# A hybrid decoder layer: scratch laid out with 32 or 128 rows outermost, more projection buffers, stores issued from GpSimd

## The chip, the cores and the metric

The kernel runs on one core of a Trainium2 chip. A core has engines that run in parallel, each through its own list of instructions in order: TensorE (PE, matrix products into the accumulator memory PSUM), VectorE (DVE), ScalarE (ACT), GpSimd (POOL) and SyncE (SP), which here only issues transfers (DMA). An instruction that waits holds up all that stand behind it on its engine. The metric is device time in microseconds (us); less is better.

## The reference

One layer over 1024 positions of 1024 channels, with 16 learned meta rows ahead (1040 in all), in float32:

```python
h_res = h_res + 0.5 * swiglu_ffn(rmsnorm(h_res, ffn1_norm), w_gate1, w_up1, w_down1)   # 1024 -> 2816 -> 1024
proj  = rmsnorm(h_res, mix_norm) @ w_in            # 1024 -> 2560
q, k, v, u = split(proj, [512, 1024, 1536])
a = diff_attention(rope(q), rope(k), v)            # 4 heads x 2 maps of 64; p0 - lam * p1; per-head norm
c = silu(layernorm(causal_depthwise_conv31(glu(u))))
h_res = h_res + concat([a, c]) @ w_out
h_res = h_res + 0.5 * swiglu_ffn(rmsnorm(h_res, ffn2_norm), w_gate2, w_up2, w_down2)
y = rmsnorm(h_res, final_norm)[16:]
```

## The kernel before

Channels lie on the 128 partitions and positions along the free axis. The sequence goes in two halves: half 1 has 528 columns (the meta rows and 512 positions, in two blocks of 264), half 2 has 512. Every product is made of three matmuls on float32r numbers: operands are split into a high and a low part (`split`, L125 to L127: the high part a copy on ScalarE, the low part a subtraction on VectorE). A weight tile of 512 KB is loaded by SyncE into `wraw` (2 buffers), and split into `whl` (4 buffers).

The stages follow one another: first feed-forward of half 1 (0 to 398 us); projections of half 1 (`project`, L600); first feed-forward of half 2, with the attention and the convolution of half 1 as pieces between its steps (`mixer`, L750); projections of half 2, with half 1's output projection inside them; second feed-forward of half 1 with half 2's attention and convolution between its steps; half 2's output projection; and half 2's second feed-forward.

`project` makes first four tiles of the convolution's gated input (L619 to L642), then the rotary keys and queries (`rope`, L649, groups of four sub-heads), then the values (L685). Keys, queries and values go through scratch in DRAM, since attention wants them in another layout. A block of keys or queries takes 48 matmuls into two PSUM tiles (`pa`, `pb`), four multiplications by the cosine and sine tables (`t`, L661), a difference and a sum (L666, L667), a split into the tile `pk` (one buffer, L654), and the store: one transfer of `pk` for keys (L674, scratch side ordered row, part, column; 128 rows outermost), four for queries (L680, each 4 sub-heads x 32 rows x columns, four outermost). Values take 24 matmuls a tile of 128 positions (`pv`), are scaled and split into `ve` (two buffers, L695 and L140/L141), and stored at L697. Attention loads the keys of a sub-head at L396, read from scratch as 4 parts x 32 rows x columns with the four outermost, the queries at L399, the values at L490. A head's score products (`sc`) go into a PSUM tile with one buffer, which the reduction of its maximum (L428) and the exponential into `p` (L437) must have read before the next one starts.

PSUM for all projections and feed-forward tiles comes from one pool of five (`psG`, L69). The sum of squares and the split of the next stage's input into `xh` and `xl` (`enter`, L279) are ordinary instructions of ScalarE and VectorE; `xh` is one buffer that each stage overwrites. Other trips through scratch: x after the first feed-forward (`xscr`, L342), the norm's factors by token (`rtok`, L614), and attention's and convolution's results (`rscr` L511, `acscr` L522).

A scheduler fixes the order on each engine before the run, from priorities and the buffers that are free. All transfers, loads and stores, are issued by SyncE in one order, so a store that waits for ScalarE's result holds up the loads behind it.

Of the kernel before, what the change touches and what calls it, by code (L numbers as in the profile page):

```python
# [9 lines left out]
F32 = mybir.dt.float32  # L10
# [39 lines left out]
def layer(ctx, tc, xb, wgu1, wd1, win, wv, wo, wgu2, wd2, colv, lamv, consts, cossin, out):  # L50
    nc = tc.nc
    V, S, T = nc.vector, nc.scalar, nc.tensor
    dma = nc.sync.dma_start

    def mm(o, lhsT, rhs, start, stop):
        T.matmul(o, lhsT, rhs, start=start, stop=stop)  # L56
# [14 lines left out]
    psB = ctx.enter_context(tc.tile_pool(name="psB", bufs=1, space=PSUM))  # L71
    dram = ctx.enter_context(tc.tile_pool(name="dscr", bufs=1, space=DRAM))

    kscr = dram.tile([4, 8, 32, L], F32, tag="kscr", name="kscr")
    qscr = dram.tile([8, 2, 64, SEQ], F32, tag="qscr", name="qscr")
    vscr = dram.tile([L, 4, 2, P], F32, tag="vscr", name="vscr")
    xscr = dram.tile([2, P, ND, HB], F32, tag="xscr", name="xscr")
    rtok = dram.tile([2, HM], F32, tag="rtok", name="rtok")
# [186 lines left out]
                        down_piece(hls[d // 2], n, d % 2, d, hs, c0, w)  # L265
                        after(c0, w, d)

# [1 line left out]
    def rms(x, c0, w):  # L269
        ssum = tmp.tile([P, 512], F32, tag="ssum", name="ssum")  # L270
        for d in range(ND):
# [58 lines left out]
    def mix_in(b, x):  # L330
        sums = {}

        def f(c0, w, d):
            if d == 0:
                sums[c0] = tmp.tile([P, 512], F32, tag="ssum", name="ssum")
            xs = x[:, d, c0:c0 + w]
            gain_piece(xs, col(C_GM + d), xh[:, d, c0:c0 + w], xl[:, d, c0:c0 + w])
            sq_piece(xs, w, sums[c0], d == 0)
            if d == ND - 1:
                norm_r(rB[:, c0:c0 + w], w, sums[c0], 95 if c0 + w == FB[b][-1][0] + FB[b][-1][1] else 60)  # L340
                a = max(c0, RO[b])
                dma(xscr[b][:, :, a - RO[b]:c0 + w - RO[b]], x[:, :, a:c0 + w])  # L342
        return f

    cst = const.tile([P, 2 * P], F32, tag="cst", name="cst")
# [18 lines left out]
        V.tensor_scalar(lnh, cols[:, C_LG:C_LG + 8], 0.5, None, op0=ALU.mult)  # L364
        V.tensor_scalar(wsub, col(C_SUB), 1.0 - LAM_INIT, None, op0=ALU.mult)

# [1 line left out]
    class Mid:  # L368
        pass

# [22 lines left out]
    def load_qk(m, sub):  # L393
        b, nk = m.b, m.nk
        k = m.qk.tile([P, nk], F32R, tag="k", name="k")
        dma(k.bitcast(F32), kscr[:, sub, :, :nk])  # L396
        q = m.qk.tile([P, 2, HB], F32R, tag="q", name="q")
        for rep in range(2):
            dma(q[64 * rep:64 * rep + 64].bitcast(F32),  # L399
                                qscr[sub, :, :, HB * b:HB * b + HB].rearrange("h r c -> r h c"))  # L400
        return k, q

    def unit(m, i, kq, ptiles, half):
# [98 lines left out]
    def sub_ln(m):  # L502
        v = psb("v")
        for h in range(4):
            sq = tmp.tile([P, 512], F32, tag="sq", name="sq")
            S.activation(sq, m.os[h], AF.Square)
            mm(v[32 * h:32 * h + 32], onesH, sq, True, True)
        rr = tmp.tile([P, 512], F32, tag="ssum", name="rr")
        rstd(v, rr, 512)
        for h in range(4):  # L510
            dma(rscr[m.b, h:h + 1], rr[32 * h:32 * h + 1])  # L511
        for h in range(4):
            ra = tmp.tile([P, 512], F32, tag="ssum", name="ra")
            dma(ra, rscr[m.b, h].partition_broadcast(P))
            V.scalar_tensor_tensor(ra, m.os[h], wsub, ra, op0=ALU.mult, op1=ALU.mult)
            store_ac(m, h, ra)

    def store_ac(m, i, src):
        hi, lo = [tmp.tile([P, HB], F32R, tag="rs", name="a") for _ in range(2)]
        split(hi, lo, src)  # L520
        for j, t in enumerate((hi, lo)):
            dma(acscr[m.b, i, :, j], t.bitcast(F32))  # L522

    def conv(m, c, z):
        a = zp.tile([P, ZH], F32, tag="z", name="acc")[:, :HB]
# [70 lines left out]
                V.tensor_tensor(x[:, d, :HB], ps, x[:, d, :HB], op=ALU.add)  # L596
                after(d)

# [1 line left out]
    def project(b, zs, between):  # L600
        es = ExitStack()
        tp = pool(es, f"tp{b}", 2)
        N = HM if b == 0 else HB
        g0 = 0 if b == 0 else HM
        ro = RO[b]
        cs = tp.tile([P, 2, N], F32, tag="cs", name="cs", bufs=1)
        dma(cs, cossin[:, :, g0:g0 + N])
        wt = WT[b]

        toks = ([(0, NM)] if b == 0 else []) + [(ro + P * t, P) for t in range(4)]  # L610
        rcol = tp.tile([P, 5], F32, tag="rcol", name="rcol", bufs=1)

        def token_rstd():
            dma(rtok[b:b + 1, :N], rB[0:1, :N])  # L614
            if b == 0:
                dma(rcol[:NM, 0:1], rtok[b, 0:NM].rearrange("(p t) -> p t", t=1))
            dma(rcol[:, len(toks) - 4:len(toks)], rtok[b, ro:N].rearrange("(t p) -> p t", p=P))

        for c in range(4):  # L619
            if c == 3:  # L620
                token_rstd()
            hg = load_w(win[2 * c + 1])
            ha = load_w(win[2 * c])
            z = zp.tile([P, ZH], F32, tag="z", name="z")
            if b == 0:
                V.memset(z[:, :ZH - HM], 0.0)
            else:
                V.tensor_copy(z[:, :CW - 1], zh[:, c])
            for c0, w in FB[b]:
                rb = rB[:, c0:c0 + w]  # L630
                pg = psg("pg")[:, :w]
                proj(pg, hg, c0, w)
                t = tp.tile([P, wt], F32, tag="t", name="t", bufs=4)[:, :w]
                V.tensor_tensor(t, pg, rb, op=ALU.mult)
                S.activation(t, t, AF.Tanh, scale=0.5)
                V.scalar_tensor_tensor(t, t, 1.0, rb, op0=ALU.add, op1=ALU.mult)
                pa = psg("pa")[:, :w]
                proj(pa, ha, c0, w)
                V.scalar_tensor_tensor(z[:, ZH - N + c0:ZH - N + c0 + w], pa, 0.5, t, op0=ALU.mult, op1=ALU.mult)
            if b == 0:  # L640
                V.tensor_copy(zh[:, c], z[:, HB:ZH])
            zs.append(z)  # L642

        between()

        for i in range(2):
            V.tensor_tensor(cs[:, i], cs[:, i], rB[:, :N], op=ALU.mult)

        def rope(wi, blocks, scale, store):  # L649
            ha = load_w(win[wi])  # L650
            hb = load_w(win[wi + 1])
            for c0, w in blocks:
                co, si = cs[:, 0, c0:c0 + w], cs[:, 1, c0:c0 + w]
                pk = tp.tile([P, 4, wt], F32R, tag="pk", name="pk", bufs=1)  # L654

                def part(hl, name):
                    ps = psg(name)[:, :w]
                    proj(ps, hl, c0, w)
                    t = [tp.tile([P, wt], F32, tag="t", name="t", bufs=4)[:, :w] for _ in range(2)]
                    for u, tab in zip(t, (co, si)):  # L660
                        V.scalar_tensor_tensor(u, ps, scale, tab, op0=ALU.mult, op1=ALU.mult)  # L661
                    return t

                ac, as_ = part(ha, "pa")
                bc, bs = part(hb, "pb")
                V.tensor_tensor(ac, ac, bs, op=ALU.subtract)  # L666
                V.tensor_tensor(bc, bc, as_, op=ALU.add)  # L667
                split(pk[:, 0, :w], pk[:, 2, :w], ac)
                split(pk[:, 1, :w], pk[:, 3, :w], bc)
                store(c0, w, pk.bitcast(F32))  # L670

        for g in range(2):
            def store_k(c0, w, pk):
                dma(kscr[:, 4 * g:4 * g + 4, :, g0 + c0:g0 + c0 + w].rearrange("k s r c -> (s r) k c"), pk[:, :, :w])  # L674

            def store_q(c0, w, pk):
                q0 = HB * b + c0 - ro
                for hl in range(2):
                    for ab in range(2):
                        dma(qscr[4 * g:4 * g + 4, hl, 32 * ab:32 * ab + 32, q0:q0 + w], pk[:, 2 * hl + ab, :w])  # L680

            rope(8 + 4 * g, FB[b], 1.0, store_k)
            rope(10 + 4 * g, QB[b], 0.125, store_q)

        for vh in range(2):  # L685
            hv = [load_w(wv[2 * vh + i]) for i in range(2)]
            for t, (c0, n) in enumerate(toks):
                ps = psg("pv")[:n, :256]
                for k in range(ND):
                    o = (k % 4) * 256  # L690
                    wh, wl = hv[k // 4][:, 0, o:o + 256], hv[k // 4][:, 1, o:o + 256]
                    mm(ps, xh[:, k, c0:c0 + n], wh, k == 0, False)
                    mm(ps, xh[:, k, c0:c0 + n], wl, False, False)
                    mm(ps, xl[:, k, c0:c0 + n], wh, False, k == ND - 1)
                ve = tp.tile([P, 2, 2, P], F32R, tag="ve", name="ve")  # L695
                gain_piece(ps.rearrange("p (a c) -> p a c", a=2), rcol[:n, t:t + 1], ve[:n, :, 0], ve[:n, :, 1])
                dma(vscr[g0 + c0:g0 + c0 + n, 2 * vh:2 * vh + 2], ve[:n].bitcast(F32))  # L697
        es.close()

    def after_out(x):  # L700
# [70 lines left out]
    def nothing(*_):  # L771
        pass

# [1 line left out]
    # keeps the tensor engine's clock up until the first operands are there  # L775
    awake = psb("awake")
    for _ in range(10):
        mm(awake[:, :P], onesD, onesD, True, True)
# [134 lines left out]
```

## Time and profile before

| | us |
|---|---|
| median of 3 runs | 2002.03 (2001.81 to 2005.81) |
| span of the profiled execution | 2003.7 |
| TensorE busy in it | 1948.8 (97%) |
| VectorE busy | 1319.8 (66%) |
| ScalarE busy | 698.6 (35%) |
| GpSimd busy | 0.2, four instructions |

The span runs from the first instruction's start to the last one's end. A busy share is over the whole span, whose stages differ: of TensorE's idle time the view by stage tells more. Rows of waits name the instruction that waited, the arrow, and what ended the wait. PEclk is the clock granted to TensorE as a share of its full speed of 2.4 GHz.

### The profile page before, as it was taken

To read this page: it belongs to the slowest core of one execution; us is meant where nothing else is said; L and a number is where in the kernel's file an instruction comes from. 1 tells how busy PE (TensorE), PEld (TensorE's weight loads), DVE (VectorE), ACT (ScalarE), POOL (GpSimd) and SP (SyncE) were. 2 spreads that over 40 slices of the span, in tenths; PEclk is the share of its full clock that TensorE was granted. 3 is DMA by queue.
4 is the path that set the end of the run, shared out by engine and by line. 5 is a ranking of instruction groups with operands and counts; after the bars stand their busy time and mean duration, and the time that the engine had idled before them with its cause. 6 is when DMAs were issued, how large, how long until landed. Compare 5 with 4: busy or idle time off the path is not lost.

```text
span 2003.7 us, 27079 instructions
## 1 busy us (share of the span) xinstructions
PE 1948.8 (97%) x10772; PEld 1682.9 (84%) x10772; DVE 1319.8 (66%) x2112; ACT 698.6 (35%) x1163; POOL 0.2 (0%) x4
## 2 busy tenths in 40 slices
PE   9999999998899999999999799999999999999997
PEld 9999999998788888788878678787878878888886
DVE  8555555766588877766565677877775684544556
ACT  5222222432343333534232444343443332222223
POOL 0000000000000000000000000000000000000000
PEclk9999999999999999999999899999999999999999
DMA  5322323354634533265425443435248343332331
GB/s 174 96 86 86 94 90 91 112 160 132 190 103 111 128 104 97 79 228 183 156 90 172 155 106 105 116 95 127 74 132 275 96 129 96 94 95 91 97 97 63
DMA packets 92947, 240.71 MB, mean 120 GB/s; under 512 B 9322, under 2 KB 26474, under 8 KB 92692
## 3 DMA queue, kind: packets, MB, share of 16 engines
q1 hardware_dynamic: 92820, 238.97, 39.9%
q8 instruction: 85, 1.39, 0.3%
q14 instruction: 42, 0.34, 0.1%
HBM read 209.43 MB, written 29.51 MB: 119 GB/s over the span
## 4 chain that ended last, share of the span: by engine, by line
PE 88%; DMA 6%; DVE 3%; ACT 2%; issue 0%; SPq 0%; ACTq 0%; DVEq 0%
PE pg L56 27%; PE pu L56 24%; PE dn L56 23%; PE wo L56 4%; PE pa L56 4%; DMA qscr<-pk 2%; PE sc L56 2%; DMA vscr<-ve 1%; DMA wraw<-wd 1%; PE o L56 1%; PE pb L56 1%; DMA kscr<-pk 1%; PE v L56 1%; PE tm L463 1%; DVE whl L127 1%; ACT whl L126 1%
## 5 line engine op out<-in xcount | busy, mean ns | idle before, releaser
L126 ACT CAST whl<-wraw 128x1024 fp32r<-128x1024 f32 (+2 forms) x329 | 337.2, 1026 | 760.6 <-PE dn L56 204.8
L56 PE MATMUL pg<-xh,whl 128*128 128x512 f32 (+1 forms) x1936 | 526.9, 352 | 12.0 <-ACT xh L126 9.5
L56 PE MATMUL dn<-h,whl 128*128 128x512 f32 (+2 forms) x2736 | 510.6, 346 | 0.0
L127 DVE TENSOR_TENSOR whl<-wraw,whl 128x1024 fp32r<-128x1024 f32 (+2 forms) x329 | 392.8, 1195 | 163.0 <-ACT whl L126 161.9
L56 PEld LDWEIGHTS dn<-h,whl 128*128 128x128 f32 x2736 | 431.8, 189 | 65.1 <-issue 1.0
L56 PE MATMUL pu<-xh,whl 128*128 128x512 f32 (+1 forms) x1744 | 475.7, 352 | 0.0
L56 PEld LDWEIGHTS pg<-xh,whl 128*128 128x128 f32 x1936 | 343.4, 190 | 63.1 <-ACT xh L126 9.9
L56 PEld LDWEIGHTS pu<-xh,whl 128*128 128x128 f32 x1744 | 308.1, 189 | 49.0 <-issue 4.2
L56 PE MATMUL pg<-xl,whl 128*128 128x512 f32 (+1 forms) x968 | 339.6, 352 | 0.0
L56 PE MATMUL pu<-xl,whl 128*128 128x512 f32 (+1 forms) x872 | 305.3, 351 | 0.0
L232 DVE SCALAR_TENSOR_TENSOR x<-dn,x 128x512 f32<-128x512 f32 (+2 forms) x248 | 139.8, 571 | 99.2 <-PE dn L56 98.8
L56 PEld LDWEIGHTS pg<-xl,whl 128*128 128x128 f32 x968 | 183.0, 190 | 24.7 <-DVE xl L127 1.1
L56 PEld LDWEIGHTS pu<-xl,whl 128*128 128x128 f32 x872 | 163.5, 188 | 22.7 <-issue 0.8
L533 DVE SCALAR_TENSOR_TENSOR acc<-z,cols,acc 128x512 f32<-128x512 f32 x240 | 179.4, 747 | 3.3
L218 DVE TENSOR_TENSOR t<-pu,t 128x512 f32<-128x512 f32 (+1 forms) x109 | 64.1, 589 | 92.3 <-PE pu L56 89.5
L210 DVE TENSOR_TENSOR t<-pg,rA 128x264 f32<-128x264 f32 (+1 forms) x65 | 33.7, 520 | 92.6 <-PE pg L56 92.6
L56 PE MATMUL pa<-xh,whl 128*128 128x264 f32 (+2 forms) x384 | 91.2, 322 | 1.7 <-DVE t L661 1.7
L56 PE MATMUL wo<-acl,whl 128*128 128x512 f32 x384 | 89.9, 395 | 0.0
L56 PEld LDWEIGHTS wo<-acl,whl 128*128 128x128 f32 x384 | 72.1, 188 | 17.5
L126 ACT CAST h<-t 128x512 fp32r<-128x512 f32 (+1 forms) x110 | 58.6, 534 | 53.8 <-DVE t L218 53.6
L56 PE MATMUL pv<-whl,xh 128*128 128x256 f32 (+1 forms) x288 | 56.7, 299 | 17.8 <-DVE ve L141 9.5
L56 PEld LDWEIGHTS pa<-xh,whl 128*128 128x128 f32 x384 | 64.6, 188 | 8.4 <-DVE t L661 1.9
(153 smaller groups left out, 1576.3 us busy)
## 6 DMA issues: line engine op xcount, KB each, us to landing
wraw<-wgu SPq DMA_DIRECT2D x175, 512.0 KB
wraw<-wd SPq DMA_DIRECT2D x64, 512.0 KB
wraw<-win SPq DMA_DIRECT2D x32, 512.0 KB
wraw<-wd SPq DMA_DIRECT2D x32, 384.0 KB
q<-qscr SPq DMA_DIRECT2D x32, 256.0 KB
acscr<-a SPq DMA_DIRECT2D x32, 256.0 KB
acl<-acscr SPq DMA_DIRECT2D x16, 512.0 KB
wraw<-wo SPq DMA_DIRECT2D x16, 512.0 KB
```

The costliest lines, as they stand in the source:

```text
L56: T.matmul(o, lhsT, rhs, start=start, stop=stop)
L126: S.copy(dst_hi, src)
L127: return V.tensor_tensor(dst_lo, src, dst_hi.bitcast(F32), op=ALU.subtract)
L210: V.tensor_tensor(tw, pg, rb, op=ALU.mult)
L218: V.tensor_tensor(tw, pu, tw, op=ALU.mult)
L232: last[0] = V.scalar_tensor_tensor(xs, m[:, :w], 0.25, xs, op0=ALU.mult, op1=ALU.add)
L463: T.transpose(tm[:, j], ps_[0][:, o:o + P], ident)
L533: V.scalar_tensor_tensor(a, z[:, j:j + HB], col(wc + j), a, op0=ALU.mult, op1=ALU.add)
```

## The change

Three things are done. The scratch of keys is now ordered sub-head, part, 32 rows, columns, and so is that of queries, so a sub-head's keys are read as 128 rows, and both are stored in four transfers a block, one for each sub-head, with 32 rows outermost. The buffers `pk` (now two) and `ve` (now four) come from a pool of their own, opened after `between()`. And all stores to scratch (`xscr`, `rtok`, `kscr`, `qscr`, `vscr`, `rscr`, `acscr`) are issued by GpSimd; loads and the kernel's output stay on SyncE. Lines after the first are one higher in the changed kernel (L54 is new), from L647 on more.

```diff
     dma = nc.sync.dma_start
+    store = nc.gpsimd.dma_start
...
-    kscr = dram.tile([4, 8, 32, L], F32, tag="kscr", name="kscr")
-    qscr = dram.tile([8, 2, 64, SEQ], F32, tag="qscr", name="qscr")
+    kscr = dram.tile([8, 4, 32, L], F32, tag="kscr", name="kscr")
+    qscr = dram.tile([8, 4, 32, SEQ], F32, tag="qscr", name="qscr")
...
-                dma(xscr[b][:, :, a - RO[b]:c0 + w - RO[b]], x[:, :, a:c0 + w])
+                store(xscr[b][:, :, a - RO[b]:c0 + w - RO[b]], x[:, :, a:c0 + w])
...
-        dma(k.bitcast(F32), kscr[:, sub, :, :nk])
+        dma(k.bitcast(F32), kscr[sub, :, :, :nk].rearrange("k r c -> (k r) c"))
...
             dma(q[64 * rep:64 * rep + 64].bitcast(F32),
-                                qscr[sub, :, :, HB * b:HB * b + HB].rearrange("h r c -> r h c"))
+                qscr[sub, :, :, HB * b:HB * b + HB].rearrange("(h a) r c -> (a r) h c", h=2))
...
-            dma(rscr[m.b, h:h + 1], rr[32 * h:32 * h + 1])
+            store(rscr[m.b, h:h + 1], rr[32 * h:32 * h + 1])
...
-            dma(acscr[m.b, i, :, j], t.bitcast(F32))
+            store(acscr[m.b, i, :, j], t.bitcast(F32))
...
-            dma(rtok[b:b + 1, :N], rB[0:1, :N])
+            store(rtok[b:b + 1, :N], rB[0:1, :N])
...
         between()
 
+        rp = pool(es, f"rp{b}", 2)
...
-        def rope(wi, blocks, scale, store):
+        def rope(wi, blocks, scale, spill):
...
-                pk = tp.tile([P, 4, wt], F32R, tag="pk", name="pk", bufs=1)
+                pk = rp.tile([P, 4, wt], F32R, tag="pk", name="pk", bufs=2)
...
-                store(c0, w, pk.bitcast(F32))
+                spill(c0, w, pk.bitcast(F32))
...
             def store_k(c0, w, pk):
-                dma(kscr[:, 4 * g:4 * g + 4, :, g0 + c0:g0 + c0 + w].rearrange("k s r c -> (s r) k c"), pk[:, :, :w])
+                for s in range(4):
+                    dst = kscr[4 * g + s, :, :, g0 + c0:g0 + c0 + w]
+                    store(dst.rearrange("k r c -> r k c"), pk[32 * s:32 * s + 32, :, :w])
 
             def store_q(c0, w, pk):
                 q0 = HB * b + c0 - ro
-                for hl in range(2):
-                    for ab in range(2):
-                        dma(qscr[4 * g:4 * g + 4, hl, 32 * ab:32 * ab + 32, q0:q0 + w], pk[:, 2 * hl + ab, :w])
+                for s in range(4):
+                    dst = qscr[4 * g + s, :, :, q0:q0 + w]
+                    store(dst.rearrange("k r c -> r k c"), pk[32 * s:32 * s + 32, :, :w])
...
-                ve = tp.tile([P, 2, 2, P], F32R, tag="ve", name="ve")
+                ve = rp.tile([P, 2, 2, P], F32R, tag="ve", name="ve", bufs=4)
                 gain_piece(ps.rearrange("p (a c) -> p a c", a=2), rcol[:n, t:t + 1], ve[:n, :, 0], ve[:n, :, 1])
-                dma(vscr[g0 + c0:g0 + c0 + n, 2 * vh:2 * vh + 2], ve[:n].bitcast(F32))
+                store(vscr[g0 + c0:g0 + c0 + n, 2 * vh:2 * vh + 2], ve[:n].bitcast(F32))
```

The order of the transfers on SyncE in half 1's projections before, from the first load of keys on (`wv` and `wgu` are weights, `k` and `q` the loads for attention; x4 means four in a row):

```order
L396 DMA k<-kscr 128x1x528
L680 DMA qscr<-pk 4x32x256 x4
L396 DMA k<-kscr 128x1x528
L680 DMA qscr<-pk 4x32x256 x2
L108 DMA wraw<-wv 128x1024
L680 DMA qscr<-pk 4x32x256 x2
L108 DMA wraw<-wv 128x1024
L399 DMA q<-qscr 64x2x512
L674 DMA kscr<-pk 128x4x264
```

And after the change:

```order
L109 DMA wraw<-win 128x1024 x8
L109 DMA wraw<-wv 128x1024 x2
L397 DMA k<-kscr 128x528 x2
L109 DMA wraw<-wv 128x1024 x2
L400 DMA q<-qscr 64x2x512 x4
L109 DMA wraw<-wgu 128x1024 x6
L491 DMA vt<-vscr 128x4x256
```

The stores are gone from this list; the loads of weights now stand with only loads of scratch between them. The stores of half 1 stand on GpSimd, after the change:

```order
L343 DMA xscr<-x 1024x1x248
L343 DMA xscr<-x 1024x1x264
L615 DMA rtok<-rB 16x1x33
L678 DMA kscr<-pk 32x4x264 x8
L684 DMA qscr<-pk 32x4x256 x8
L678 DMA kscr<-pk 32x4x264 x8
L684 DMA qscr<-pk 32x4x256 x8
L701 DMA vscr<-ve 16x512
L701 DMA vscr<-ve 128x512 x4
```

There were none on this engine before. The second place is the end of half 2's projections on ScalarE. Before, with `ve` the values' high part, `xh` the feed-forward's input, `th` the tanh of the first gate tile and `p` the exponential of the scores:

```order
L140 ACTIVATE ve<-pv,rcol 128x2x128 x4
L126 CAST xh<-xs 128x512 x3
L126 CAST whl<-wraw 128x1024 x2
L140 ACTIVATE ve<-pv,rcol 128x2x128
L126 CAST xh<-xs 128x512 x5
L126 CAST whl<-wraw 128x1024
L437 ACTIVATE p,sm<-sc,nm 128x656
L207 ACTIVATE th<-pg 128x512
```

And after the change:

```order
L127 CAST xh<-xs 128x512 x4
L127 CAST whl<-wraw 128x1024
L208 ACTIVATE th<-pg 128x512
L141 ACTIVATE ve<-pv,rcol 128x2x128 x4
L127 CAST whl<-wraw 128x1024
L127 CAST h<-t 128x512
L127 CAST whl<-wraw 128x1024
L208 ACTIVATE th<-pg 128x512
L127 CAST whl<-wraw 128x1024
L127 CAST h<-t 128x512
L438 ACTIVATE p,sm<-sc,nm 128x656
```

The last four `ve` have moved behind the first gate tile's `th`, and the first exponential `p` behind the second gate tile's `h`. On VectorE at the same place, after the change (`acc` are convolution steps, `t<-th,pg` the gate's product):

```order
L209 SCALAR_TENSOR_TENSOR t<-th,pg 128x512
L534 SCALAR_TENSOR_TENSOR acc<-z,cols,acc 128x512 x2
L142 SCALAR_TENSOR_TENSOR ve<-pv,rcol,ve 128x2x128
L534 SCALAR_TENSOR_TENSOR acc<-z,cols,acc 128x512
L142 SCALAR_TENSOR_TENSOR ve<-pv,rcol,ve 128x2x128 x2
```

Before, the last `ve` there stood among the low parts of `xh`, ahead of all convolution steps; now two of these and the gate's product stand ahead of the first of the last four.

## Rows read from the trace of the kernel before

**Rows 1.** The page, busy time: engine, us (share of the span) and instructions.

```profile
PE 1948.8 (97%) x10772; PEld 1682.9 (84%) x10772; DVE 1319.8 (66%) x2112; ACT 698.6 (35%) x1163; POOL 0.2 (0%) x4
```

**Rows 2.** Windows, three stages: us, busy (count) per engine, clock, DMA share, GB/s.

```profile
460.00:545.00 85.00, 72.51 (x548) 68.00 (x548) 45.85 (x97) 23.74 (x44) 0.00 (x0) 0.94 0.55 171
...
1030.00:1130.00 100.00, 83.48 (x420) 71.21 (x419) 55.94 (x84) 27.19 (x40) 0.00 (x0) 0.90 0.49 154
1130.00:1475.00 345.00, 334.78 (x1615) 276.48 (x1613) 272.69 (x405) 146.96 (x260) 0.00 (x0) 0.99 0.40 109
```

**Rows 3.** Windows, stretches at half clock: the first, the last, the sum of seven.

```profile
499.50:502.91 3.41, 3.21 (x16) 2.17 (x17) 2.54 (x6) 0.00 (x0) 0.00 (x0) 0.50 0.98 291
...
1376.73:1380.14 3.41, 3.41 (x10) 2.67 (x9) 3.41 (x5) 0.93 (x3) 0.00 (x0) 0.50 0.70 161
sum 37.52, PE 30.19 PEld 24.80 DVE 26.58 ACT 19.10 POOL 0.00; mean PE 4.31 PEld 3.54 DVE 3.80 ACT 2.73 POOL 0.00
```

**Rows 4.** Waits of TensorE, 460 to 545 us: total us, times, longest.

```profile
PE pg L56 <- ACT xh L126: 5.9, 1, 5.9
PE pv L56 <- DVE t L661: 4.9, 1, 4.9
```

**Rows 5.** Waits of TensorE, 1030 to 1130 us.

```profile
PE pv L56 <- DVE ve L141: 9.5, 1, 9.5
PE pg L56 <- ACT xh L126: 3.6, 1, 3.6
```

**Rows 6.** Waits of TensorE, 1130 to 1475 us.

```profile
PE sc L56 <- ACT p L437: 10.2, 3, 3.8
```

**Rows 7.** Waits of ScalarE, 460 to 545 us.

```profile
ACT pk L126 <- DMA qscr<-pk: 21.7, 3, 9.1
ACT pk L126 <- DMA kscr<-pk: 12.4, 3, 4.3
```

**Rows 8.** Waits of ScalarE, 1030 to 1130 us.

```profile
ACT ve L140 <- DMA vscr<-ve: 19.4, 3, 13.4
```

**Rows 9.** The chain that ended last: start us, us, what was waited for.

```profile
470.08 4.96 DMA kscr<-pk
478.05 8.76 DMA qscr<-pk
...
1180.82 13.95 DMA wraw<-wd
```

**Rows 10.** DMA issues: destination, source, queue, count, KB each.

```profile
k<-kscr SPq DMA_DIRECT2D x8, 520.0 KB
...
kscr<-pk SPq DMA_DIRECT2D x4, 528.0 KB
...
qscr<-pk SPq DMA_DIRECT2D x16, 128.0 KB
```

**Rows 11.** Timeline of ScalarE: start us, us, instruction, [idle before, releaser].

```profile
419.05 0.63 ACT L131 ACTIVATE ssum<-x 128x512 f32<-128x512 f32 x1 [2.96 <-DMA x<-xb]
...
443.01 1.05 ACT L126 CAST whl<-wraw 128x1024 fp32r<-128x1024 f32 x1 [4.96 <-PE pg L56]
...
1185.17 0.59 ACT L207 ACTIVATE th<-pg 128x512 f32<-128x512 f32 x1
...
1194.85 1.05 ACT L126 CAST whl<-wraw 128x1024 fp32r<-128x1024 f32 x1 [6.43 <-DMA wraw<-wd]
1195.80 0.61 ACT L126 CAST h<-t 128x512 fp32r<-128x512 f32 x1
```

**Rows 12.** Windows, two blocks of keys in the first projections.

```profile
449.51:461.13 11.62, 11.62 (x98) 11.62 (x97) 11.09 (x19) 3.16 (x5) 0.00 (x0) 1.00 0.29 85
```

**Rows 13.** Timeline of VectorE at 1186 us.

```profile
1186.44 0.68 DVE L208 SCALAR_TENSOR_TENSOR t<-th,pg 128x512 f32<-128x512 f32 x1
```

**Rows 14.** The page, groups: VectorE convolution steps, busy, mean ns, idle before.

```profile
L533 DVE SCALAR_TENSOR_TENSOR acc<-z,cols,acc 128x512 f32<-128x512 f32 x240 | 179.4, 747 | 3.3
```

**Rows 15.** SyncE, issues of the stores of q: ns least/median/most, first to last.

```profile
L680 SPq DMA_DIRECT2D qscr<-pk x24: 503/552/4317, 475.8 to 1096.8; - x24
```

## The prediction

> **What bounds the kernel now.** I read the busy table first. TensorE is busy 1948.8 us of the span, so at most the rest and the cost of a halved clock can be won by anything but fewer matmuls; GpSimd does four set-up instructions and nothing else [rows 1]. Next the span by stage: TensorE's idle time lies in three places, 85.00 − 72.51 = 12.5 us at the end of half 1's projections (A, 460 to 545 us), 100.00 − 83.48 = 16.5 us at half 2's (B, 1030 to 1130), and 345.00 − 334.78 = 10.2 us in half 2's attention (C, 1130 to 1475) [rows 2]. After such gaps the granted clock falls to half (1.2 of 2.4 GHz); there are seven such stretches, 37.52 us in all, with TensorE busy for 30.19 us of them [rows 3]. At full clock that work takes half, so they cost 15.1 us (A 4.0, B 7.7, C 3.4).
>
> Then the waits, stage by stage. In A TensorE waits for the casts of xh, the operand of the next feed-forward, and for the rotary products t [rows 4]; in B for ve, which frees the PSUM of the values, and again for xh [rows 5]; in C three times, 10.2 us together, for the exponential p that frees the score PSUM [rows 6]. None of these is itself a slow engine. ScalarE in A waits 21.7 us for the stores of q to land and 12.4 us for those of k, because there is one pk buffer [rows 7]; in B 19.4 us for the stores of v, of whose buffer ve there are two [rows 8]. The chain of waits shows why a landing is late: 128 KB of q takes 8.76 us where 528 KB of k takes 4.96 us, and in C a weight of 512 KB that was issued behind a 520 KB load of k takes 13.95 us [rows 9, 10]. ScalarE's cast of that weight stood 6.43 us, and the exponential stands behind that cast [rows 11].
>
> **What the slow transfers have in common.** In the code each slow one has the dimension of size four outermost on one side (q's store 4x32xw, k's load 4x32xnk); the fast ones begin with 128 rows. By rows, four q stores of 128 KB from 478.05 on, with two k loads about, took longer than a k store of four times the size [rows 9, 10]. After the change all these begin with 32 or 128 rows. The Trainium skill (DMA: Bandwidth & Descriptors, "Why a DMA increments its semaphore by 16 and not by 1") has a transfer use the largest number of engines up to 16 that divides the slowest dimension of both its sides, so four before and sixteen now; by that rule the waits of C go, without it they stay (R3), and the durations in the rows side with it.
>
> **The change part by part.**
>
> Two pk buffers and stores that land in about 5 us [rows 9] take the pk waits away: a buffer is now needed again after two blocks, 11.62 us in half 1 [rows 12]. Four ve buffers do it for the values. SP's queue no longer holds stores that wait for ScalarE; the value and feed-forward weights stand there only behind loads of k and q, whose stores are of the first four sub-heads and done some 25 us earlier (four blocks of 5.8 us [rows 12]). In C the k load with 128 rows should land like the k store of its size, 4.96 us [rows 9], and the weight behind it not 9 us late; the wait of 6.43 us ends. What goes at most is all idle time of A, B and C and its clock: 12.5 + 16.5 + 10.2 + 15.1 = 54.3 us.
>
> What stays, as an estimate:
> - A: xh of the next feed-forward may be written only after the last value matmul has read it. Its first cast takes 0.61 us [rows 11], the low part on VectorE about as long, and the next pairs follow at the matmuls' pace: 2.0 us with some clock.
> - B: the order has changed. On ScalarE the last four ve now stand behind th of the first gate tile. With five PSUM buffers, pg and four values fill them, so pu starts when the first of these ve is done: th 0.59 us [rows 11], on VectorE t 0.68 [rows 13] and two convolution steps of 0.747 us that stand ahead [rows 14], and ve itself, which I put at 0.45: 3.2 us; and for a clock halved once more 1.7 us, half of the 3.41 us that the short stretches last [rows 3].
> - B and C: half 2's first head now begins about two gate-up pairs later, and its score and transposition steps stand closer together on TensorE. Each step needs a reduce, an exponential and casts in turn, with such convolution steps between [rows 14]. Eleven such steps at some 0.45 us each: 5 us, my least certain term, from half such a convolution step; it lies between nothing and three whole ones a step, 25 us.
> - C: 0.5 us for a first load of a head.
>
> Together 12.4 us, so 54.3 − 12.4 = 41.9 us are won. On the profiled execution's span of 2003.7 us that is 1961.8; the median shown before is 2002.03, 1.7 us under that span, so I forecast 1960 us.
>
> **The price of GpSimd's queue.** It is idle before, so no row has a store from it. Each block of keys or queries now issues four stores there, in order. From below, SP spent 503 ns on the quickest issue of a q store, median 552, and from above 4317 on the slowest [rows 15]. I take 0.55 us, nearest to most of these: 2.2 us for four. It is hidden as long as four fit into a block: half 1's block is 11.62 / 2 = 5.8 us [rows 12], so up to 1.4 us a store cost nothing; half 2's blocks are twice as wide and bear about twice that. Beyond it, half 1's 32 stores of k and q run over by 32T − 8 × 5.8 − 6 (the second buffer and the values behind give the last 6): 18 us at T = 2.2, 41 us at 2.9. Below 0.55 nothing is won. The Trainium skill (DMA: Bandwidth & Descriptors, "Specifications") gives a first byte of about 1 us from GpSimd against 0.6 from SP; by that ratio 0.55 would be an estimate of 0.92 us, still hidden.
>
> The wide store of x to scratch (1024 rows) also goes there. The input of half 2 used to be issued behind it on SP, and ScalarE's squares wait 2.96 us for that input [rows 11]. This input takes the place of the x that is being stored, so it still waits for the store's end; a store that ends some microseconds later is hidden by ScalarE's slack in the projections that follow, where it stands 4.96 us at once for TensorE [rows 11]. The store's own reader comes hundreds of us later. The small stores of norms are hidden by the feed-forward; TensorE's order there is the same.
>
> **Rivals.**
>
> R1, GpSimd is too slow: between T = 1.9 and 2.5 the gain of A and part of the rest go back, at T = 2.2 1960 + 18 = 1978, with something in B 1981. From T = 2.9 on the 41 us eat the whole gain and the kernel is slower, by 2 us at T = 3.0 and by 44 at 4.3, the row's upper end (32 x 4.3 − 52.4 = 85, less 41), so 2004 to 2046: pk would then wait for the landing of a store that waits in GpSimd's queue, TensorE for the rotary products. For it speaks that SP itself needed 4317 ns once [rows 15]; against it that this was a queue full of earlier small transfers, and the median 552. The Trainium skill (SBUF — State Buffer, "DVE blocks DMA") has GpSimd's descriptor writing stand still while VectorE runs certain fast copies; here VectorE in these stretches mostly combines two operands, and no row can show it; it would be one way to such a T.
>
> R2, the later attention jams: if VectorE, with its convolution steps, can't serve the closer steps of half 2's first head, each costs two to three convolution steps and the 5 us become 22: 1977. For it: VectorE is busy 272.69 of 345.00 us in C [rows 2], the fullest it gets. Against: it is busy for only 79% of that stretch, and the new order leaves 10 to 16 feed-forward matmuls between the steps.
>
> R3, C's waits stay: the weight is late for the 520 KB ahead of it, not for how these are spread. Then 13.6 us (10.2 + 3.4) come back: 1975. For it: the load of k is as large as the weight. Against: two transfers of about 520 KB at the k store's pace take 10 us, not 14 [rows 9].
>
> R4, nothing is kept back: 2002.0 − 54.3 = 1948.
>
> **How the numbers follow.** Forecast 0.60 (own range 1950 to 1975); R1 0.07 for about 1981, 0.03 for a T just under 2.9 that leaves the time where it was, and 0.07 for slower; R2 0.08; R3 0.07; R4 0.08. About 0.2% or 4 us is what a measurement of this kernel can tell from no change. So slower is R1's far end, 0.07; the same 0.03; faster all the rest, 0.90. The range of 8 in 10 takes in R4's edge, R2, R3 and R1's near end: 1948 to 1985. The far end of R1 is left out.
>
> **What would show it.** In the profile after: no wait of ScalarE's pk or ve for DMA above 1 us; TensorE's gap to the score PSUM in C under 1 us for each head, and the weight behind the k load landing in about 5 us; A's idle time at about 2 us, B's at about 5 with pu waiting for ve; at most three halved stretches before 1200 us. GpSimd's stores following each other closer than 1.4 us. R1 would show as pk waiting for kscr or qscr with stores 2 us and more apart on GpSimd; R2 as sc and tm waiting for p and pts between 1150 and 1240 us; R3 as the old wait of the whl cast for wd. I am wrong in the mechanism if the waits go but TensorE's busy time grows by as much.

## The result and the profile after

The changed kernel takes 1957.43 us (median of 4 runs, 1956.22 to 1958.79) against 2001.92 us (1999.54 to 2005.81) of the kernel before: a ratio of 0.9763, 95% interval 0.9739 to 0.9788. The forecast was 1960 us, range 1948 to 1985.

The busy table of the page, to be held against [rows 1]:

```profile
span 1956.8 us, 27152 instructions
PE 1935.3 (99%) x10772; PEld 1671.9 (85%) x10772; DVE 1318.3 (67%) x2112; ACT 699.3 (36%) x1163; POOL 61.0 (3%) x115
```

The span is 46.9 us shorter, and TensorE's busy time 13.5 us with the same number of matmuls: that is the clock. The other 33.4 us are idle time. The three stages, which now lie 45 us earlier by the end, and as a last row the one stretch left at half clock behind the start (columns as in [rows 2]):

```profile
460.00:534.00 74.00, 74.00 (x574) 70.40 (x573) 49.54 (x106) 27.05 (x51) 22.78 (x42) 1.00 0.68 208
1020.00:1095.00 75.00, 71.32 (x395) 61.46 (x394) 56.23 (x83) 27.08 (x40) 11.44 (x21) 0.98 0.56 165
1095.00:1430.00 335.00, 333.43 (x1619) 274.33 (x1619) 270.35 (x404) 145.65 (x258) 1.61 (x3) 1.00 0.41 121
1091.97:1095.38 3.41, 3.36 (x8) 2.69 (x9) 3.38 (x7) 0.09 (x1) 0.76 (x2) 0.50 0.87 262
```

A, the end of half 1's projections, has no idle time left (74.00 of 74.00, before 12.5 us); B has 3.7 us (before 16.5), C 1.6 us (before 10.2). What TensorE waits for, in the whole execution (us in total, times, longest):

```profile
PE pu L57 <- DVE t L209: 3.0, 1, 3.0
PE pg L57 <- ACT xh L141: 1.8, 2, 1.4
PE sc L57 <- DMA q<-qscr: 1.6, 1, 1.6
PE awake L57 <- DVE onesD L91: 1.1, 1, 1.1
PE v L57 <- DVE ssum L136: 1.0, 1, 1.0
```

The waits of [rows 4 to 6] are gone; the wait of `pu` and that of `sc` for q are new, and the other three stand at the kernel's two ends. Two shorter new ones lie between: `dn` for VectorE, 0.8 us at 863 us, and in B `pg` for the low part `xl`, 0.7 us at 1086 us. On ScalarE no `pk` waits for a transfer any more; of all projection waits for scratch in [rows 7, 8] one kind is left, two waits of which the longer is 4.9 us, and it holds nothing up:

```profile
ACT ve L141 <- DMA vscr<-ve: 5.6, 2, 4.9
```

The transfers (KB each, median us to landing) and GpSimd's issues of the new stores (count, busy us, mean ns, idle before):

```profile
wraw<-wd SPq DMA_DIRECT2D x64, 512.0 KB, 3.6
...
k<-kscr SPq DMA_DIRECT2D x8, 520.0 KB, 3.8
...
kscr<-pk POOLq DMA_DIRECT2D x16, 132.0 KB, 3.7
...
qscr<-pk POOLq DMA_DIRECT2D x16, 128.0 KB, 3.9
```

```profile
L678 POOL DMA_DIRECT2D kscr<-pk x24 | 13.1, 553 | 154.7 <-DVE pk L128 154.7
L684 POOL DMA_DIRECT2D qscr<-pk x24 | 13.0, 550 | 32.3 <-DVE pk L128 32.3
```

A load of k lands in 3.8 us, a weight of 512 KB in 3.6 us where one behind a load of k took 13.95 us before, and a q store in 3.9 us where 8.76 us stood in the chain before [rows 9]; and T, the issue on GpSimd whose price no row of before could give, is 0.55 us, the value chosen.

### The profile page after: what moved, and what is told of

Same layout as the page of the kernel before. It is cut to its first block, busy times and chain, and to the rows that moved or that the text cites. A ratio compares the mean times of both kernels' runs of the same rounds, so it can differ in the third digit from the quotient of the medians.

```text
span 1956.8 us, 27152 instructions
## 1 busy us (share of the span) xinstructions
PE 1935.3 (99%) x10772; PEld 1671.9 (85%) x10772; DVE 1318.3 (67%) x2112; ACT 699.3 (36%) x1163; POOL 61.0 (3%) x115
## 4 chain that ended last, share of the span: by engine, by line
PE 95%; DVE 2%; issue 1%; DMA 1%; ACT 0%; POOL 0%; SPq 0%; DVEq 0%; ACTq 0%; POOLq 0%
PE pg L57 27%; PE pu L57 24%; PE dn L57 24%; PE pa L57 5%; PE wo L57 4%; PE pv L57 3%; PE pb L57 2%; PE sc L57 2%; PE o L57 2%; PE tm L464 1%; PE v L57 1%; DVE whl L128 0%; DMA q<-qscr 0%; PE both L57 0%; DMA acscr<-a 0%
## 5 line engine op out<-in xcount | busy, mean ns | idle before, releaser
L128 DVE TENSOR_TENSOR h<-t,h 128x512 fp32r<-128x512 f32 (+1 forms) x110 | 63.9, 583 | 10.1 <-ACT h L127 9.8
L438 ACT ACTIVATE p<-sc,nm 128x144 f32<-128x144 f32 (+7 forms) x64 | 48.1, 752 | 62.9 <-DVE nm L429 57.0
```

Of the source, the lines that this page charges most:

```text
L128: return V.tensor_tensor(dst_lo, src, dst_hi.bitcast(F32), op=ALU.subtract)
L438: S.activation(p[:, lo:nk].rearrange("p (n w) -> p n w", n=n), sc[:, 0:n, :w], AF.Exp, bias=nmc, accum_out=smc)
```

## The experiments

The kernel before was run beside each on the same chip, and each ratio is to that; two kernels are compared by their ratios, and a difference of ratios is given in us of the kernel before. The change has three parts: the layout, the buffers, GpSimd's queue. Four runs undo or strain one part of the changed kernel, five do parts alone.

**Stores back on SyncE.**

```diff
-    store = nc.gpsimd.dma_start
+    store = nc.sync.dma_start
```

> The changed kernel with all stores to scratch issued from SyncE again; layout and buffers stay new. Theory 1 (the stores' landing time and the buffers were the wait, the queue only little): about 1962 us, A (460 to 534 us) idle under 3 us, C as in the changed kernel, since SyncE needs about 0.55 us for an issue as GpSimd does and the next weights stand at most one block behind. Theory 2 (the queue was the wait, loads stood behind stores that wait for ScalarE): about 1985 us, with casts of whl waiting for wraw in A and B.

Measured: 1967.26 us, ratio 0.9800 (0.9785 to 0.9815), so the queue is worth 0.4%, some 7 us, to the changed kernel. Theory 1 holds in size. In A TensorE idles 2.9 us up to 534 us, as was said, and 4.0 us up to 545, and in B the order has a second wait of `pu` of 3.0 us.

**One pk, two ve.**

```diff
-name="pk", bufs=2)   ... name="ve", bufs=4)
+name="pk", bufs=1)   ... name="ve", bufs=2)
```

> The changed kernel with one pk buffer and two ve buffers, as before the change; layout and GpSimd's queue stay new. Theory 1 (landing in 4 to 5 us after 2.2 us of issues is about one block of half 1, 5.8 us): pk waits for kscr and qscr return in A, some 1 to 2 us a block, and ve waits for vscr in B: 1965 us, 1962 to 1972. Theory 2 (the buffers were the wait): A and B back to 12 and 16 us idle with their clock, about 1990 us.

Measured: 1977.96 us, ratio 0.9856 (0.9840 to 0.9872): the buffers are worth 0.93%, 19 us, between the two theories. A idles 8.0 us and B (here 1030 to 1135 us) 8.7. ScalarE waits for a q store only once, 7.9 us, and for no store of the values, yet waits of 1 to 5 us of TensorE come back with their clock. How each of them comes from the buffers wasn't followed.

**The old layout.**

```diff
-    kscr = dram.tile([8, 4, 32, L], ...)      qscr = dram.tile([8, 4, 32, SEQ], ...)
+    kscr = dram.tile([4, 8, 32, L], ...)      qscr = dram.tile([8, 2, 64, SEQ], ...)
...  (loads and stores of k and q as before, stores from GpSimd)
```

> The changed kernel with the scratch of keys and queries laid out and moved as before (four outermost in q's stores and k's loads), stores from GpSimd, two pk and four ve. Theory 1: C's waits for the weight behind the 520 KB load of k come back in full, 10.2 us of idle time and 3.4 us of clock, so about 1971 us, and A stays without pk waits above 2 us thanks to the second buffer. Theory 2 (R3: not the spread but the volume): C as in the changed kernel, 1957 us.

Measured: 1979.35 us, ratio 0.9862 (0.9842 to 0.9881), 20 us lost against the changed kernel, 14 expected. In A TensorE idles 0.3 us, though one wait of `pk` for a store of q is left, 6.0 us where at most 2 were said. C's waits are back, and so is the chain (start us, us, what was waited for; the first is B's):

```profile
1095.82 13.95 DMA k<-kscr
...
1157.32 13.44 DMA wraw<-wd
1243.73 14.21 DMA wraw<-wd
1332.11 14.51 DMA wraw<-wd
```

```profile
PE sc L57 <- DMA q<-qscr: 10.7, 2, 9.3
PE sc L57 <- ACT p L438: 10.5, 3, 4.4
```

10.5 us in three waits are those of [rows 6]. The further 10.7 us show the same cause in another place: half 2's first head needs its q at once, and q is issued behind a load of k that takes 13.95 us. R3 (volume) is refuted: the volume is the same in both kernels.

**Three more stores behind each of k and q.**

```diff
                     store(dst.rearrange("k r c -> r k c"), pk[32 * s:32 * s + 32, :, :w])
+                    for _ in range(3):
+                        store(dum[1][dum[0]], pk[32 * s:32 * s + 32, 0, :128])
+                        dum[0] += 1
```

> The changed kernel with three small extra stores (32 rows of 512 bytes of the same tile, to a scratch of their own) behind each store of k and q: GpSimd has 16 issues a block instead of 4, about 8.7 us where half 1's block lasts 5.8 us and half 2's 11.1 us. By the prediction's formula with T = 4 x 0.54 = 2.16 us: half 1 overruns by 32 x 2.16 - 46.4 - 6 = 17 us, half 2 by nothing, so about 1974 us. Rival: GpSimd's queue is not on the path even so (the scratch is wanted late), 1957 to 1960 us.

Measured: 1989.73 us, ratio 0.9903 (0.9878 to 0.9928), 28 us above the changed kernel, forecast 17. The issues (columns as above) and where TensorE then waits:

```profile
L681 POOL DMA_DIRECT2D dum<-pk x72 | 35.7, 501 | 133.4 <-ACT pk L128 128.6 <-DMA dum<-pk 4.6 <-issue 0.2
```

```profile
PE pv L57 <- DVE ve L143: 14.7, 1, 14.7
...
PE pv L57 <- DVE t L664: 3.9, 1, 3.9
```

The overrun is there and TensorE stands 14.65 + 3.90 = 18.6 us for it in half 1, as the formula has it (17); what it left out is the clock, 20.48 us at half with 9.07 us of matmuls in them, so 4.5 us more, and a second wait of `pu` in B of 3.0 us. So GpSimd's queue is off the path only as long as a block's issues fit into the block, and the rival, that nothing waits for it, is wrong.

**Each part alone, from the kernel before.** The edits are the ones above turned round: the layout of k and q (the stores in four transfers, from SyncE), the pool `rp` with its two and four buffers, and `store` on GpSimd.

> The kernel before with the new scratch layout of keys and queries alone (stores on SyncE, one pk, two ve). Theory 1 (the spread of the transfers is worth C's 13.6 us anywhere, and in A and B q lands in 4 to 5 us instead of 8.8, so half of the pk waits go, some 10 us): 24 us under the kernel before, ratio 0.988. Theory 2 (with one pk buffer the store's landing holds the block anyway): only C's 13.6 us, ratio 0.993.

> The kernel before with two pk and four ve in a pool of their own alone (stores on SyncE, old layout). Theory 1 (two buffers cover a landing of 8.8 us, as two blocks of half 1 last 11.6 us): A's and B's idle time and clock, 16.5 and 24.2 us, shrink to about 15 together, C stays: 25 us under before, ratio 0.9875. Theory 2 (loads queued behind stores and the four-engine q stores on SyncE hold A up anyway): under 8 us, ratio 0.996 to 1.

> The kernel before with all stores to scratch issued from GpSimd alone (old layout, one pk, two ve). Theory 1 (the queue is the smallest of the three parts, as putting the stores back on SyncE cost the changed kernel 0.4%): about 7 to 10 us under before, ratio 0.9955, C unchanged. Theory 2 (q's old stores land sooner from GpSimd, 5 to 9 us and spread over more engines, so that A's pk waits go with them): 20 us under, ratio 0.99.

| part alone | us | ratio to before | 95% interval |
|---|---|---|---|
| layout | 1980.54 | 0.9887 | 0.9862 to 0.9912 |
| buffers | 1972.63 | 0.9846 | 0.9820 to 0.9871 |
| GpSimd's queue | 2010.31 | 1.0033 | 1.0021 to 1.0044 |

*Layout.* The size is theory 1's, the place is not: C's waits go (TensorE busy 344.37 of 345.00 us) and B's idle time falls to 8.8 us, but A keeps its own, 11.6 us. The stages A, B and C of this run:

```profile
460.00:545.00 85.00, 73.45 (x553) 68.95 (x552) 49.01 (x97) 24.61 (x43) 0.00 (x0) 0.96 0.54 163
1030.00:1130.00 100.00, 91.20 (x469) 77.61 (x468) 66.47 (x96) 30.59 (x43) 0.00 (x0) 0.95 0.49 147
1130.00:1475.00 345.00, 344.37 (x1663) 282.46 (x1662) 280.81 (x420) 156.47 (x276) 0.00 (x0) 1.00 0.37 117
```

In A the waits of `pk` for stores of k are gone, but two for stores of q are left, although these land in 2.3 us at the median. The landing that ended the first of the two took 5.01 us, and with one buffer the next block stood for it:

```profile
ACT pk L126 <- DMA qscr<-pk: 15.5, 2, 7.8
```

```profile
qscr<-pk SPq DMA_DIRECT2D x16, 128.0 KB, 2.3
```

*Buffers.* Theory 1, and more of it: A falls to 2.0 us idle, with the old slow stores on the old queue. Of B's 9.6 us, 8.8 are one wait of `sc` for q behind the slow load of k; C keeps 7.6 of its 10.2 us.

```profile
460.00:545.00 85.00, 83.02 (x609) 76.78 (x608) 59.76 (x122) 31.24 (x60) 0.00 (x0) 1.00 0.59 191
1030.00:1130.00 100.00, 90.44 (x481) 77.14 (x480) 68.72 (x101) 33.45 (x52) 0.00 (x0) 0.97 0.59 177
1130.00:1475.00 345.00, 337.42 (x1622) 277.50 (x1621) 272.16 (x407) 150.75 (x265) 0.00 (x0) 0.99 0.39 110
```

```profile
PE sc L57 <- DMA q<-qscr: 8.8, 1, 8.8
```

*GpSimd's queue alone makes the kernel slower*, which neither theory had. ScalarE's waits for the stores, and the cost of an issue:

```profile
ACT pk L127 <- DMA qscr<-pk: 40.3, 4, 16.5
ACT ve L141 <- DMA vscr<-ve: 35.9, 7, 12.0
ACT pk L127 <- DMA kscr<-pk: 22.6, 6, 8.8
```

```profile
L682 POOL DMA_DIRECT2D qscr<-pk x24 | 16.6, 698 | 37.4 <-ACT pk L127 36.6 <-DVE pk L128 0.8
L676 POOL DMA_DIRECT2D kscr<-pk x6 | 4.7, 789 | 179.3 <-DVE pk L128 179.3
```

An issue of an old-layout store takes 0.70 us (q) or 0.79 us (k) here, where SyncE took 0.55 us for q [rows 15] and 0.38 us for k:

```profile
L674 SPq DMA_DIRECT2D kscr<-pk x6: 376/377/382, 464.3 to 1084.8; - x6
```

With one buffer the next block waits for issue and landing, ten times in twelve blocks. `pk`'s waits for k grow most against the kernel before, from 14.7 us to 22.6; those for q were 38.3 us there.

**Whether k and q make that loss.**

```diff
-    store(kscr[:, 4 * g ...      store(qscr[4 * g ...
+    dma(kscr[:, 4 * g ...        dma(qscr[4 * g ...
```

> As the run with GpSimd's queue alone (old layout, one pk, two ve), but k and q are stored from SyncE; the other stores stay on GpSimd. Theory 1 (that run was 0.33% slower than before because GpSimd needs 0.69 to 0.79 us to issue an old-layout store of k or q, and with one pk buffer each block waits for issues and landing): the loss goes, ratio 0.998 to 1.000. Theory 2 (the loss is in the values, norms or wide stores): it stays, ratio 1.003.

Measured: 2001.61 us, ratio 0.9986 (0.9976 to 0.9997). The loss goes with the k and q stores; the other stores on GpSimd cost nothing. Whether it is the issue's 0.15 us (q) and 0.41 us (k) more or the landing is not separated.

**The layout of the keys alone**, from the kernel before (`kscr` and its load and stores as in the change, `qscr` as it was):

> The kernel before with the scratch of keys alone in the new layout (loads of k with 128 rows outermost, k stored in four transfers from SyncE). Theory 1: C's three waits of 2.7 to 3.8 us before the score products go with their clock, 13.6 us, ratio 0.993. Theory 2 (R3, volume and not spread): C unchanged, ratio 1.00.

Measured: 1990.08 us, ratio 0.9933 (0.9910 to 0.9955), as theory 1 said. C (columns as above), which starts 5 us later here, has no idle time at all, at full clock:

```profile
1135.00:1480.00 345.00, 345.00 (x1670) 284.26 (x1669) 282.69 (x423) 154.88 (x272) 0.00 (x0) 1.00 0.36 113
```

That the whole agrees too is in part a balance: A idles 15.6 us (before 12.5) and B, to 1135 us, 12.9 (before 16.5).

**Two steps further.** The changed kernel was run again beside them.

> The changed kernel as it is, on the same chip as the next two, to compare them with: ratio to the kernel before 0.976.

```diff
-                ve = rp.tile([P, 2, 2, P], F32R, tag="ve", name="ve", bufs=4)
+                ve = rp.tile([P, 2, 2, P], F32R, tag="ve", name="ve", bufs=7)
```

> The changed kernel with seven ve buffers instead of four; the order then puts three of the last four ve ahead of the casts of xh, so that PSUM tiles are free before the first gate tile ends. Theory 1 (pu's wait of 2.99 us at 1089 us is for PSUM, which pg and four values not yet scaled hold): that wait and the half clock behind it (3.41 us, 1.7 us of work) go, 4.7 us, ratio to the changed kernel 0.9976. Theory 2 (pu waits for something else, or the wait comes back at xh): no difference.

And besides that:

```diff
-        dma(k.bitcast(F32), kscr[sub ...
+        with tc.high_priority(offset=AHEAD):
+            dma(k.bitcast(F32), kscr[sub ...
...  (the loads of q, and the values' gain_piece, likewise)
```

> As the run before, and the loads of k and q for attention, and the scaling of the values, with a higher priority in the scheduler, so that a head's loads stand ahead of the weights on SyncE. Theory 1: head 0 of half 2 no longer waits 1.6 us for its q, 6.3 us in all, ratio to the changed kernel 0.9968. Theory 2: the weight loads are now late behind 1 MB of k and q, and casts of whl wait: 2 us lost against the run before.

Measured: the changed kernel 1957.75 us (1956.81 to 1958.56), with seven `ve` 1955.40 (1954.89 to 1956.30), with the early loads too 1952.47 (1951.51 to 1955.72); ratios to before 0.9768, 0.9757, 0.9746 (0.9727 to 0.9764). With seven `ve` the wait of `pu` is gone, as theory 1 had it, but another order gives 2.3 us back at half 1's first head and 1.2 us at `wo`. Nor was there a halved clock to win: in the changed kernel's run beside it the same wait of 2.99 us is followed by full clock (1.00 from 1092.70 to 1096.11 us). So the gain is half of what was said. With the early loads these and the wait for q go as well, 5.3 us in all against 6.3 forecast, and this version is faster than both kernels; its five times all lie under the changed kernel's four. TensorE's longest waits in it, all at the start but the last, at the end:

```profile
PE pg L57 <- ACT whl L127: 1.1, 1, 1.1
PE awake L57 <- DVE onesD L91: 1.1, 1, 1.1
PE pg L57 <- ACT xh L141: 1.1, 2, 0.9
PE v L57 <- DVE ssum L136: 1.0, 1, 1.0
```

## Why the prediction was right, step by step

**Where the time was.** Right. The changed kernel lost the idle time of A, B and C and the halved clock behind it; the matmuls are the same. Of 54.3 us that could go, 46.9 went from the span.

**That the waits for stores come from slow landing and too few buffers.** Right, with the parts now sized: the buffers alone give 1.54%, the layout alone 1.13%, together (stores on SyncE) 2.00%. They overlap. A was almost wholly the buffers': it idles 2.0 us with them alone, 11.6 us with the layout alone and 8.0 us with the layout and GpSimd's queue but one `pk`. So a quicker landing without the second buffer didn't clear A, though the prediction named the slow landing beside the single buffer there. In B the layout and the buffers alone each about halve the idle time, to 8.8 and 9.6 us, and what is left with the buffers is the wait for q behind the slow load of k.

**C and R3.** Right: with the key scratch alone C's idle time is gone, and the whole gains 0.67% (forecast 13.6 us, 0.68%); the old layout put into the changed kernel brings the three waits back at 10.5 us (before 10.2).

**The price of GpSimd's queue.** Right in size, but partly by luck: 0.55 us was chosen and 0.55 measured, yet the row it came from is SyncE's price for the old stores of q. GpSimd takes 0.70 us for those, and SyncE 0.43 us for the new ones (first row, the layout alone, ns least/median/most; second row, the changed kernel):

```profile
L682 SPq DMA_DIRECT2D qscr<-pk x24: 303/432/977, 484.5 to 1127.0; - x24
```

```profile
L684 POOL DMA_DIRECT2D qscr<-pk x24: 550/550/553, 472.6 to 1069.7; - x24
```

GpSimd's 24 issues lie within 3 ns of one another beside a busy VectorE, so the stall that R1 named as a way to a long T did not come. SyncE's issue of 4317 ns, which the prediction put down to small transfers ahead of it, stood 2.4 us behind the issue of a 520 KB load of k, with a weight of 512 KB and two stores of 256 KB between; what made it long no run shows. At T = 2.9 R1's formula gives 40.4 us, not 41. The overrun formula gave 17 us for four times as many issues, and 18.6 us of standing time were measured; the formula missed the clock behind such a gap. What the prediction did not see is that T depends on the transfer's shape: 0.55 us for the new stores, 0.70 and 0.79 for the old ones, 0.91 for the wide store of x; and that the queue's value has a sign that hangs on the rest: 0.33% lost alone, 0.4% won with the other two parts.

**What stays.** Here the terms were mis-sized: 12.4 us were put down, and 54.3 − 46.9 = 7.4 us stayed.
- A, 2.0 us: measured 0.
- B, `pu`: 3.2 us forecast, 2.99 us measured and 1.7 us of clock as said, but by another path; and in a second profile of the same kernel (two steps further) no halved clock followed the same wait. These are ScalarE and VectorE at that time, and `pu`'s first matmul:

```profile
1089.06 1.05 ACT L127 CAST whl<-wraw 128x1024 fp32r<-128x1024 f32 x1 [2.95 <-PE pg L57]
1090.01 0.59 ACT L208 ACTIVATE th<-pg 128x512 f32<-128x512 f32 x1
```

```profile
1090.14 1.23 DVE L128 TENSOR_TENSOR whl<-wraw,whl 128x1024 fp32r<-128x1024 f32 x1
1091.28 0.68 DVE L209 SCALAR_TENSOR_TENSOR t<-th,pg 128x512 f32<-128x512 f32 x1
...
1093.33 0.48 DVE L142 SCALAR_TENSOR_TENSOR ve<-pv,rcol,ve 128x256 fp32r<-128x256 f32 x1
```

```profile
1092.02 0.79 PE L57 MATMUL pu<-xh,whl 128*128 128x512 f32 x1 [2.99 <-DVE t L209]
```

`pu` starts when `t` ends, 1.3 us before the low part of the first late `ve` begins. The prediction counted five tiles and had the values' four released first; but the fifth is `pg` itself, and `t`, its last reader, frees it before any `ve` does. What made it late was the split of a weight that stands between: its cast on ScalarE (1.05 us) ahead of `th`, its low part on VectorE (1.23 us) ahead of `t`. The sum came out alike by chance. Seven `ve` took the wait away, as PSUM is then free sooner.
- The later attention, 5 us: measured nothing. TensorE waits there neither for VectorE nor for ScalarE, so it didn't jam, and R2 is refuted.
- C, 0.5 us for a first load of a head: 1.57 us, of `sc` for a q whose second load stood on SyncE behind a weight. It is all of C's idle time.
- Not foreseen: `pg` waits 0.7 us in B for the low part `xl`, and a product `dn` of half 2's first feed-forward waits 0.8 us at 863 us for VectorE. The runs with stores on GpSimd show 0.3 to 1.3 us there, the one with the stores back on SyncE none. In the chain before `dn` stands a store of the results, issued by GpSimd, on which VectorE waited 3.46 us ahead of the step that `dn` wants (first row: start us, us, what was waited for; second row: ScalarE's waits for such stores in the whole execution):

```profile
855.08 5.80 DMA acscr<-a
```

```profile
ACT a L127 <- DMA acscr<-a: 53.4, 13, 7.6
```

ScalarE and VectorE together wait 88.4 us for these stores, before 23.7, and 23.1 with the stores back on SyncE: moving them to GpSimd had a price, which other work hid but for this 0.8 us.

So the result lies 2.6 us under the forecast by the medians, on the side of R4 (nothing kept back), and 5.0 us by the spans of the profiled executions (12.4 − 7.4); the attention term's 5 us are the larger part of what was put down too much. Of the signs that the prediction named two failed: ScalarE still waits up to 4.9 us for a store of `ve`, where 1 us was the bound, and `pu` waits for `t` and not for `ve`. Neither changes where the time went.

## What to carry over

When an engine waits for stores to land, look at both cures: a second buffer gives a landing the time of two blocks instead of one (here 11.62 us; with the buffers alone the old landings, 8.76 us in the chain before, left A 2.0 us of idle time), and an outer dimension of 32 or 128 rows instead of 4 shortens it. In A the second buffer was what paid; in C, where a load of k held up a weight on one queue, only the layout cleared it. An idle queue isn't free: its issue time counts by block, and moving all stores to it alone made this kernel 0.33% slower, while with the other two parts it gave 0.4%. When PSUM holds a product back, list all tiles of the pool with their last readers, the product's own predecessor too, and take the one that ends first.

## What was not expected of the hardware

An issue on GpSimd took a time of its own for each shape: 0.49 us for a single row (`rscr`), 0.50 for 32 rows of 512 bytes, 0.55 for 32 x 4 runs, 0.70 for the old stores of q with as many runs but 4 outermost, 0.79 for 128 x 4, 0.91 for the 1024 runs of x. And stores with four rows outermost, slow from SyncE, are the slower ones from GpSimd too: with the queue alone changed a median landing of 5.2 us (128 KB) and 11.4 us (256 KB), against 3.9 and 4.8 us with 32 rows outermost in the changed kernel. Nor does a gap of one length always halve TensorE's clock: behind the same wait of 2.99 us two executions of the changed kernel show 0.50 and 1.00.
